# Two loading queues in the head of a two-layer GELU kernel, and three stores cut in halves

## The chip, the cores and the metric

The kernel runs on one core of one Trainium2 chip. The metric is the device time in microseconds (us). Each execution also has a span, from the first to the last instruction of the program. The device time is the span plus something outside it.

## The reference

```python
x: 16 x 512 x 768, w1: 768 x 3072, b1: 3072, w2: 3072 x 768, all float32
y = np.matmul(x, w1) + b1
y = 0.5 * y * (1.0 + erf(y / np.sqrt(2.0)))      # exact GELU
return np.matmul(y, w2).astype(np.float32)
```

## The kernel before

Both products are done with Strassen-like sums of blocks in float16. Nearly all of the run is one unbroken stream of matmuls.

The **head** loads the first four row tiles of x and the first weight tile in float32. SyncE issues them; VectorE casts them to float16. Each x tile is 128 x 768 x 4 bytes (384 KB), each half of the weight tile is as large.

```python
        for t in range(4):
            nc.sync.dma_start(out=xf[:, t, :], in_=xr[:, t, :])
        wts[0] = slots[0]
        for half in range(2):
            r = slice(half * KQ, (half + 1) * KQ)
            nc.sync.dma_start(out=wf[:, r, :], in_=w1r[:, r, 0:2 * P])
        nc.scalar.dma_start(out=bf, in_=b1.rearrange("(hc p) -> hc p", p=P))
        ...
        nc.gpsimd.tensor_copy(out=xh_of(0, 4)[:, 0:1], in_=xf[:, 0, 0:1])   # GpSimd waits for x tile 0
        load_wt(1)                       # then loads, casting on the way: the second weight tile,
        for t in range(4, 8):            # x tiles 4 to 7, and more weight tiles
            load_x(0, t)
        ...
        spin(9)                          # nine matmuls on zeros: warm-up filler for TensorE
        for t in range(4):
            xhs[t] = xh_of(0, t)
            nc.vector.tensor_copy(out=xhs[t], in_=xf[:, t, :])              # cast
            transpose_pe(0, t, copy_halves if t == 3 else nc.scalar.copy)   # 6 transposes, ScalarE copies
            if t == 0:
                nc.tensor.transpose(out=bW[:, 0:2 * NH], in_=bf, ...)       # the bias
            spin(2)
        for r, c in (...):               # three casts of the weight tile: first half in two, then the second
            nc.vector.tensor_copy(out=w1_raw(wts[0])[:, r, c], in_=wf[:, r, c])
        # ... the matmuls of the first weight tile ("plain") follow
```

The **stores** of parts of W2 (for later use) wait in a list; `drain` issues some of them at each slot of a row unit of the second product:

```python
        def raw_w2(p):
            b11, _, b21, b22 = quarters(p)
            for n, b in ((1, b11), (2, b21), (3, b22)):
                raws.append(lambda p=p, n=n, b=b: nc.sync.dma_start(out=w2s[p, n][:], in_=b))
        ...
            drain(slot, 3 if U == 0 and slot > 1 else int(U + 1 == NU))
```

The **end**: the last two pieces of output are stored by SyncE and ScalarE, one each:

```python
                (nc.sync, nc.scalar)[t].dma_start(out=orr[:, self.sb * 8 + 2 + t, N2:N2 + N4], in_=o)
```

After it, SyncE waits for every DMA semaphore that is in use. The DMAs of SyncE and ScalarE take eight semaphores in a cycle.

Of the kernel before, what the change touches and what calls it, by code (L numbers as in the profile page):

```python
# [10 lines left out]
P = 128  # L11
# [11 lines left out]
def kernel(  # L23
# [8 lines left out]
    nc = tc.nc  # L32
# [10 lines left out]
    NU = RH // P  # L43

    xr = x.rearrange("b (s p) k -> p (b s) k", p=P)
    orr = out.rearrange("b (s p) n -> p (b s) n", p=P)
    w1r = w1.rearrange("(kc p) c -> p kc c", p=P)
    w2r = w2.rearrange("(hc s p) n -> p s hc n", s=2, p=P)

    NQ = NH // 2  # L50
# [8 lines left out]
    w2s = {(p, q): dp.tile([P, NQ, N4], F16, name=f"w2s{p}{q}")  # L59
           for p in range(1, 8) for q in range(1, 8)}  # L60
# [28 lines left out]
    def cut(off, n, pattern=None, **dims):  # L89
        ap = arena[:, off:off + n]  # L90
        return ap.rearrange(pattern, **dims) if pattern else ap
# [23 lines left out]
    def wt_at(off):  # L115
        return cut(off, WT_N)
# [14 lines left out]
    slots = dict(enumerate([wt_at(o_wt + k * WT_N) for k in range(3)] + [wt_at(o) for o in o_far]))  # L131
# [73 lines left out]
    with tc.manual_schedule():  # L205
# [9 lines left out]
        def sums(ns):  # L215

            for q in (soon, queue):
                while q and ns >= q[0][0] * 0.6:
                    ns -= q[0][0]
                    q.pop(0)[1]()  # L220

        def flush(q):
            while q:
                q.pop(0)[1]()


        wts = {}
# [36 lines left out]
        puts, raws, LAG = [], [], [2]  # L264

        def quarters(p):
            w = w2v[SLOT[p]]
            return w[:, 0, 0:NQ, :], w[:, 1, 0:NQ, :], w[:, 0, NQ:NH, :], w[:, 1, NQ:NH, :]

        def split_w2(p, t, q=None, ns=(7, 5, 6, 4)):  # L270

            b11, b12, b21, b22 = quarters(p)

            def put(q, src, eng=nc.sync):
                eng.dma_start(out=w2s[p, q][:], in_=src)

            t = {n: spare[k] for n, k in zip((7, 5, 6, 4), t)}
            for n, a, b in ((7, b22, b12), (5, b12, b11), (6, b22, t[5]), (4, b21, t[6])):
                def f(n=n, a=a, b=b):
                    tt(t[n], a, b, SUB)  # L280
                    puts.append([LAG[0], lambda eng: put(n, t[n], eng)])
                if n in ns:
                    later(WB, f, slow if q is None else q)
# [5 lines left out]
        def raw_w2(p):  # L289
            b11, _, b21, b22 = quarters(p)  # L290
            for n, b in ((1, b11), (2, b21), (3, b22)):
                raws.append(lambda p=p, n=n, b=b: nc.sync.dma_start(out=w2s[p, n][:], in_=b))

        ORDER = (1, 6, 2, 7, 5, 4, 3)
        w2_order = [(ORDER[0], q) for q in (1, 2, 5, 6)]
# [53 lines left out]
        def g_sum(k, U, c0=0, c1=NH, q=None):  # L349
            G1, G2 = g_of(U // NU)  # L350
            r = slice(U % NU * P, (U % NU + 1) * P)
            g11, g21 = G1[:, c0:c1, 0, r], G1[:, c0:c1, 1, r]
            g12, g22 = G2[:, c0:c1, 0, r], G2[:, c0:c1, 1, r]
            s = [t[:, c0:c1, :] for t in GS]
            a, b, op = ((g21, g22, ADD), (s[0], g11, SUB), (g11, g21, SUB), (g12, s[1], SUB))[k]
            later((c1 - c0) * P, lambda: tt(s[k], a, b, op), q)
# [27 lines left out]
        def lev_sums(i, c0=0, c1=NQ, ks=(0, 1, 2, 3), q=None, m=None):  # L384

            A = OPERAND[ORDER[i]] if m is None else operand(*HYBRID[m])
            levs = None if m is None else hyb_lev[m]
            a11, a12 = A[:, c0:c1, 0:2 * P], A[:, NQ + c0:NQ + c1, 0:2 * P]
            a21, a22 = A[:, c0:c1, 2 * P:RH], A[:, NQ + c0:NQ + c1, 2 * P:RH]
            s = [t[:, c0:c1, :] for t in (lev_of(i) if levs is None else levs)]  # L390
            for k in ks:
                a, b, op = ((a21, a22, ADD), (s[0], a11, SUB), (a11, a21, SUB),
                            (a12, s[1], SUB))[k]
                later((c1 - c0) * 2 * P, lambda k=k, a=a, b=b, op=op: tt(s[k], a, b, op), q)
# [344 lines left out]
        xf = cut(GR, 8 * K).bitcast(FP32).rearrange("p (t k) -> p t k", t=4)  # L739
        wf = cut(GR + 8 * K, 8 * KQ * P).bitcast(FP32).rearrange("p (k c) -> p k c", c=2 * P)  # L740
        bf = cut(GR + 8 * K + 8 * KQ * P, 2 * P).bitcast(FP32)[0:2 * NH, :]
        idf = cut(GR + 8 * K + 8 * KQ * P + 2 * P, 2 * P).bitcast(FP32)
        assert 8 * K + 8 * KQ * P + 4 * P <= GR // 2
        for t in range(4):
            nc.sync.dma_start(out=xf[:, t, :], in_=xr[:, t, :])
        wts[0] = slots[0]
        for half in range(2):
            r = slice(half * KQ, (half + 1) * KQ)
            nc.sync.dma_start(out=wf[:, r, :], in_=w1r[:, r, 0:2 * P])
        nc.scalar.dma_start(out=bf, in_=b1.rearrange("(hc p) -> hc p", p=P))  # L750
        zero = XTs[1][:, 0]
        nc.vector.memset(zero[:, 0, :], 0.0)
        nc.scalar.activation(out=zero[:, 1, 0:1], in_=zero[:, 0, 0:1], func=GELU)
# [204 lines left out]
        def drain(slot, n=0, eng=nc.sync, wait=True):  # L958
            for f in puts:
                f[0] -= 1  # L960
            while puts and not (wait and puts[0][0] > 0):
                puts.pop(0)[1](eng)
            for f in raws[:n]:
                f()
            del raws[:n]

        def fill_mm2_one(sb, U, slot):
            if slot == 1:
                flush(queue)
                g_sum(2, U, q=soon)  # L970
                if U == 0:
                    g_sum(3, U, q=soon)
                flush(soon)
                if U == 0:
                    for p in (1, 2, 3, 5, 6, 7, 4):
                        raw_w2(p)
                    w4 = (6, 4, 5, 3)
                    split_w2(4, w4, ns=(5, 6, 4))
                    split_w2(1, (0, 1, 2, 6))
                    split_w2(2, (3, 0, 1, 2))  # L980
                    split_w2(4, w4, ns=(7,))
            drain(slot, 3 if U == 0 and slot > 1 else int(U + 1 == NU))
            if slot == 2:
                soon.extend(late)
                late.clear()
                if U + 1 < NU:
                    g_sum(0, U + 1, q=soon)
            if slot == 3 and U > 0:
                g_sum(3, U, q=soon)
            if slot == 4 and U + 1 < NU:  # L990
                g_sum(1, U + 1, q=soon)
            if U + 2 == NU and slot == 5:
                lev_sums(None, m=0, ks=(0, 1, 3))
            if U + 1 == NU and slot == 4:
                lev_sums(None, m=0, ks=(2,))
            if slot > 1:
                sums(1200)
            if slow and (U and slot > 1 or slot > 4):
                slow.pop(0)[1]()
                if slow and slot == 6:  # L1000
                    slow.pop(0)[1]()
            if slot == 6 and U + 1 == NU:
                flush(slow)
                flush(queue)
# [131 lines left out]
        for g, (kind, sb, k) in enumerate(units):  # L1136
            if g < 2:
                loads_a(g)
                if g:
                    transposes_a(g)  # L1140
                continue
            cur = kind(g, sb, k)
            if g < len(seq):
                period(cur, prev, lambda slot: fill_a(g, slot))
            else:
                f = {Unit1: fill_mm1, Unit2: fill_lean if sb else fill_mm2_one, UnitH: fill_hyb,
                     Unit3: fill_mm2_two}[kind]
                period(cur, prev, lambda slot: f(sb, k, slot))
            prev = cur
# [30 lines left out]
```

## Time and profile before

| what | value |
|---|---|
| time, median of the first three runs | 852.35 us (851.21 to 852.37) |
| profiled execution: time, span | 850.89, 848.7 us |
| TensorE busy | 843.3 us, 99% |
| first real matmul (line L788) | 9.39 us |
| end of TensorE to end of the span | 3.86 us |
| TensorE gaps after 9.39 us | none in busy time (the ends of matmuls are modelled; by their starts, one wait of 0.1 us at 10.8) |

To read it: a kernel whose TensorE is 99% busy can win only before its first real matmul, after its last one, or in gaps of the stream. The last two rows and the first matmul are those three places. The prediction shows the lines.

### The profile page before, as it was taken

The numbers are of one execution on the slowest core, as the hardware profiler recorded it, in microseconds if no ns is written. First come the engines' busy times: TensorE is split into PE (matmuls) and PEld (weight loads), VectorE is DVE, ScalarE is ACT, GpSimd is POOL, SyncE is SP. The second block draws the span as 40 slices with busy tenths as digits, with TensorE's granted clock in tenths as the row PEclk, the third lists the DMA queues.
The fourth block names the chain that finished last, engine by engine and source line by source line (L and its number), as shares of the span: only waits on it lengthen the run. The fifth ranks groups of instructions, "written<-read, shape, count | busy, mean of one in ns | idle before, by whom it ended". The sixth has DMA issues, their size and how long they took to land.

```text
span 848.7 us, 16767 instructions
## 1 busy us (share of the span) xinstructions
PE 843.3 (99%) x6546; PEld 577.6 (68%) x6546; DVE 673.5 (79%) x1134; ACT 426.4 (50%) x700; POOL 94.9 (11%) x151
## 2 busy tenths in 40 slices
PE   9999999999999999999999999999999999999998
PEld 5444445796544897449964499545995469964798
DVE  5766679777857997679967799668996699957997
ACT  4777763231287413773247721587116761277611
POOL 5021100042200002000020000200002100010000
PEclk9999999999999999999999999999999999999999
DMA  9998796699998699987999489994999949984397
GB/s 228 216 274 166 166 221 232 233 201 221 361 329 206 207 341 370 255 201 259 335 368 300 118 296 346 359 276 123 319 356 335 281 114 324 369 300 168 106 308 282
DMA packets 144819, 222.11 MB, mean 262 GB/s; under 512 B 61964, under 2 KB 85444, under 8 KB 144740
## 3 DMA queue, kind: packets, MB, share of 16 engines
q1 hardware_dynamic: 117392, 178.85, 66.4%
q0 software_dynamic: 27168, 42.08, 22.4%
q8 instruction: 51, 0.84, 0.4%
q14 instruction: 28, 0.23, 0.1%
q10 hardware_dynamic: 180, 0.11, 0.0%
HBM read 181.78 MB, written 49.45 MB: 272 GB/s over the span
## 4 chain that ended last, share of the span: by engine, by line
PE 99%; DMA 1%; SPq 0%; DVE 0%; ACT 0%; issue 0%
PE bY L416 22%; PE bY L520 15%; PE bX L416 14%; PE bX L520 10%; PE bZ L416 7%; PE bW L416 7%; PE bZ L520 5%; PE bW L520 5%; PE bY L459 4%; PE bZ L459 2%; PE bW L459 2%; PE bY L608 2%; PE bX L608 1%; PE bX L459 1%; DMA arena<-in_x_dram 1%; PE bZ L608 1%
## 5 line engine op out<-in xcount | busy, mean ns | idle before, releaser
L210 DVE TENSOR_TENSOR arena<-arena 128x1536 f16<-128x1536 f16 (+6 forms) x638 | 409.8, 674 | 4.8 <-DMA arena<-arena 0.7
L416 PEld LDWEIGHTS <-arena 128*128 128x128 f16 x2016 | 196.6, 98 | 220.1 <-issue 0.5
L520 PEld LDWEIGHTS <-arena 128*128 128x128 f16 x3528 | 292.1, 98 | 8.2
L416 PE MATMUL bY<-arena 128*128 128x512 f16 (+1 forms) x864 | 214.5, 375 | 0.0
L639 DVE TENSOR_TENSOR arena<-bY,arena 128x512 f32<-128x512 f32 (+1 forms) x102 | 69.4, 680 | 118.2 <-PE bY L416 88.3
L632 ACT COPY bY<-bX 128x512 f32<-128x512 f32 (+1 forms) x145 | 79.6, 549 | 118.1 <-DVE arena L569 87.8
L520 PE MATMUL bY<-arena 128*128 128x192 f16 x1500 | 138.3, 246 | 0.0
L416 PE MATMUL bX<-arena 128*128 128x512 f16 (+1 forms) x576 | 138.3, 375 | 0.0
L432 ACT ACTIVATE arena<-arena,b1t 128x1024 f16<-128x1024 f32 x94 | 108.0, 1149 | 51.6 <-DVE arena L667 51.6
L652 ACT COPY arena<-bW 128x512 f32<-128x512 f32 (+1 forms) x149 | 81.9, 550 | 93.1 <-PE bW L520 43.9
L520 PE MATMUL bX<-arena 128*128 128x192 f16 x1020 | 93.1, 246 | 0.0
L667 DVE TENSOR_TENSOR arena<-bZ,arena 128x512 f32<-128x512 f32 (+1 forms) x102 | 69.2, 679 | 22.3 <-PE bZ L416 19.1
L416 PE MATMUL bZ<-arena 128*128 128x512 f16 (+1 forms) x288 | 76.2, 375 | 0.0
L416 PE MATMUL bW<-arena 128*128 128x512 f16 (+1 forms) x288 | 76.2, 375 | 0.0
L552 POOL DMA_DIRECT2D out_dram<-arena x42 | 30.5, 728 | 403.1 <-DVE arena L663 367.5
L683 ACT COPY bZ<-bY 128x512 f32<-128x512 f32 (+1 forms) x60 | 31.8, 529 | 80.8 <-PE bY L459 30.0
L437 ACT ACTIVATE arena<-bX,b1t 128x512 f16<-128x512 f32 x94 | 64.0, 681 | 9.8 <-PE bX L416 9.7
L437 ACT ACTIVATE arena<-bY,b1t 128x512 f16<-128x512 f32 x94 | 63.3, 674 | 0.0
L459 PEld LDWEIGHTS <-arena 128*128 128x128 f16 x432 | 42.2, 98 | 28.0 <-issue 0.2
L319 POOL DMA_DIRECT2D arena<-in_x_dram x60 | 33.7, 635 | 161.7 <-DMA arena<-arena 153.4
L520 PE MATMUL bZ<-arena 128*128 128x192 f16 x504 | 48.4, 246 | 0.0
L520 PE MATMUL bW<-arena 128*128 128x192 f16 x504 | 48.4, 246 | 0.0
(63 smaller groups left out, 426.8 us busy)
## 6 DMA issues: line engine op xcount, KB each, us to landing
arena<-w2s SPq DMA_DIRECT2D x299, 288.0 KB, 4.8
arena<-w1s SPq DMA_DIRECT2D x72, 672.0 KB, 7.0
out_dram<-arena POOLq DMA_DIRECT2D x46, 384.0 KB, 7.1
w2s<-arena SPq DMA_DIRECT2D x49, 288.0 KB, 4.5
arena<-in_x_dram POOLq DMA_DIRECT2D x60, 192.0 KB, 7.6
w1s<-arena SPq DMA_DIRECT2D x12, 672.0 KB, 5.9
arena<-in_w_dram POOLq DMA_DIRECT2D x17, 384.0 KB, 8.6
out_dram<-arena SPq DMA_DIRECT2D x13, 384.0 KB, 2.5
```

What stands on the lines that cost most here:

```text
L210: nc.vector.tensor_tensor(out=o, in0=a, in1=b, op=op)
L319: nc.gpsimd.dma_start(out=xhs[t], in_=xr[:, sb * 8 + t, :])
L416: nc.tensor.matmul(out=dst[:, r:r + w], lhsT=w1_op(self.wt, slot)[:, c, :], rhs=a[:, c, r:r + w], start=first and c == 0 and r == 0, stop= ...
L432: nc.scalar.activation(out=self.G[1][:, hi, :, :], in_=self.tmp, func=GELU, bias=b1t[:, 2 * hi + 1:2 * hi + 2])
L437: nc.scalar.activation(out=self.G[0][:, hi, row, :], in_=bank[:, 0:RH], func=GELU, bias=b1t[:, 2 * hi:2 * hi + 1])
L459: nc.tensor.matmul(out=dst[:, 0:N2], lhsT=a, rhs=w[:, :, c, :], start=first and c == 0, stop=c == self.C - 1, skip_group_check=True)
L520: nc.tensor.matmul(out=dst[:, t * N4:(t + 1) * N4], lhsT=a, rhs=w[:, c, :], start=first and c == 0 and t == ts[0], stop=c == NQ - 1, skip_ ...
L608: nc.tensor.matmul(out=dst[:, t * N4:(t + 1) * N4], lhsT=a, rhs=self.w[q][:, c, :], start=first and c == 0 and t == 0, stop=c == NQ - 1, s ...
L632: nc.scalar.copy(out=bY[u.g % 2][:, 0:u.F], in_=bX[u.g % 2][:, 0:u.F])
L639: nc.vector.tensor_tensor(out=u.c22(), in0=bY[u.g % 2][:, 0:u.F], in1=w[:, 0:u.F], op=ADD)
L652: nc.scalar.copy(out=w[:, 0:u.F], in_=bW[:, 0:u.F])
L667: nc.vector.tensor_tensor(out=u.c12(), in0=bZ[:, 0:u.F], in1=w[:, 0:u.F], op=ADD)
```

## The change

The intent is a shorter head: x tiles 1 and 3 and the second half of the weight tile are issued by ScalarE while SyncE issues the others. Three of the raw W2 stores (those of product 4) go out in halves, two pieces per slot.

```diff
             for n, b in ((1, b11), (2, b21), (3, b22)):
-                raws.append(lambda p=p, n=n, b=b: nc.sync.dma_start(out=w2s[p, n][:], in_=b))
+                for c in (slice(0, NQ // 2), slice(NQ // 2, NQ)) if p == 4 else (slice(0, NQ),):
+                    raws.append(lambda p=p, n=n, b=b, c=c: nc.sync.dma_start(out=w2s[p, n][:, c, :],
+                                                                             in_=b[:, c, :]))
 ...
+        wts[0] = slots[0]
+        pair = (nc.sync, nc.scalar)
         for t in range(4):
-            nc.sync.dma_start(out=xf[:, t, :], in_=xr[:, t, :])
-        wts[0] = slots[0]
+            pair[t % 2].dma_start(out=xf[:, t, :], in_=xr[:, t, :])
+            if t == 1:
+                nc.scalar.dma_start(out=bf, in_=b1.rearrange("(hc p) -> hc p", p=P))
         for half in range(2):
             r = slice(half * KQ, (half + 1) * KQ)
-            nc.sync.dma_start(out=wf[:, r, :], in_=w1r[:, r, 0:2 * P])
-        nc.scalar.dma_start(out=bf, in_=b1.rearrange("(hc p) -> hc p", p=P))
+            pair[half].dma_start(out=wf[:, r, :], in_=w1r[:, r, 0:2 * P])
 ...
-            drain(slot, 3 if U == 0 and slot > 1 else int(U + 1 == NU))
+            drain(slot, 3 if U == 0 and slot > 1 else 2 * int(U + 1 == NU))
```

## The prediction

> **What bounds the kernel now.** I read the page first (busy time, then the chain that ended last), then that chain in order of time for the first 30 us, then the timeline of VectorE, ScalarE and the DMA issues, then the busy time by stretches.
>
> ```profile
> PE 843.3 (99%) x6546; PEld 577.6 (68%) x6546; DVE 673.5 (79%) x1134; ACT 426.4 (50%) x700; POOL 94.9 (11%) x151
> ...
> PE 99%; DMA 1%; SPq 0%; DVE 0%; ACT 0%; issue 0%
> ```
>
> TensorE is busy 843.3 us of a span of 848.7, so 5.4 us are not matmuls. In the trace's TensorE records I find 1.19 us before its first instruction, 3.86 us after its last (the final sum and stores), and three gaps of 0.17, 0.09 and 0.14 us, all before 9.39 us. From 9.39 us to 844.9 us there is no gap at all. Part of the busy time before 9.39 us is filler ("spin" matmuls on zeros), so the real margin is the head, and only the head:
>
> ```profile
> 2.14 5.54 DMA arena<-in_x_dram
> 7.68 0.02 issue
> 7.70 0.57 DVE arena L772
> 8.27 0.05 issue
> 8.32 0.52 PE bT L333 x6
> 8.84 0.02 issue
> 8.87 0.49 ACT arena L329
> 9.35 0.04 issue
> 9.39 0.81 PE bX L788 x3
> ```
>
> These are pieces of the chain: start, duration, what. The reader is to see that x row tile 3 lands at 7.68, is cast (0.57), transposed (0.52), copied by half (0.49), and the first real matmul starts at 9.39. A second path arrives at the same moment:
>
> ```profile
> 4.03 0.56 DVE L772 CAST arena<-arena 128x768 f16<-128x768 f32 x1 [2.89 <-DMA arena<-in_x_dram]
> 4.98 0.92 DVE L772 CAST arena<-arena 128x768 f16<-128x768 f32 x1 [0.39 <-DMA arena<-in_x_dram]
> 6.67 0.56 DVE L772 CAST arena<-arena 128x768 f16<-128x768 f32 x1 [0.77 <-DMA arena<-in_x_dram]
> 7.70 0.56 DVE L772 CAST arena<-arena 128x768 f16<-128x768 f32 x1 [0.47 <-DMA arena<-in_x_dram]
> 8.81 1.92 DVE L780 CAST arena<-arena 128x384 f16<-128x384 f32 x3 [0.55 <-DMA arena<-in_w_dram]
> ```
>
> From VectorE's timeline: x tiles 0 to 3 land at about 4.00, 4.96, 6.64 and 7.68 (each cast starts 0.02 to 0.03 later), the first half of W1 tile 0 at 8.79; the trace has the second half at 9.87. The first weight cast (0.43 us) ends at 9.24, so the weight path is ready some 0.1 us before the x path. Both bind. The six loads are 384 KB each (393 kB).
>
> What limits those landings is not the issue. SyncE issues the six in 0.41 to 0.49 us each, 0.74 to 3.58 us, while the first lands at 4.00. The stretches show the transfer rate:
>
> ```profile
> 2.50:4.50 2.00, 2.00 (x6) 0.70 (x5) 0.47 (x1) 0.37 (x2) 0.44 (x1) 1.00 1.08 397
> 4.50:6.50 2.00, 2.00 (x17) 1.22 (x16) 1.01 (x2) 0.82 (x2) 2.00 (x4) 1.00 0.94 300
> 6.50:8.50 2.00, 1.74 (x18) 0.75 (x16) 1.12 (x2) 1.53 (x3) 2.00 (x4) 1.00 1.05 369
> ```
>
> Last two columns: DMA share and GB/s. The engines are full from 2.5 us (share 0.94 or more). One 3072-byte packet takes 121 ns in the packet records, so 16 engines give 16 x 3072 / 121 = 406 GB/s: the 397 seen is the limit. Between 4.5 and 6.5 us some packets take 300 to 1100 ns and the rate falls to 300, a loss of (397 - 300) x 2 us = 194 kB or 0.5 us.
>
> **What the Trainium skill says.** (1) "DMA: Bandwidth & Descriptors", section "Issuing engines are not separate DMA queues": initiating DMAs on several engines only saves the sequencer's time to initiate them. The trace agrees in that 6 issues of 0.45 us are 2.7 us in all and end well before the data. (2) Same page, "Queues, rings and completion order": each DMA engine takes the queue rows it has work for in turn, a packet at a time. The trace of before can't show it for SyncE against ScalarE (ScalarE's only early load is 12 KB of bias). For SyncE against GpSimd it does not agree: GpSimd's first load, issued at 4.57, has its first packet at 8.60, when SyncE's are running out. (3) "ScalarE: Activation LUTs", "What ACT_TABLE_LOAD costs": about 1283 ns; the trace has 1.28 us. (4) "TensorE: Matmul & The Clock Gate", "Part 1": after an idle window of about 3.4 us the clock halves. Before, no idle comes near that.
>
> **The change, part by part.**
>
> *Head, issue.* ScalarE now issues x1, the bias, x3 and the second weight half: 3 x 0.45 + 0.62 us, with 0.05 between, from 0.73 to about 2.8 us. Its table load then moves from 1.39 to about 2.8 and ends near 4.1, with the tiny GELU 4.3; ScalarE's first copy is at 5.68 before. This costs nothing. SyncE's last head issue ends at about 2.1 instead of 3.58; nothing waited for it. Saving on the path: at most the start-up. Before 2.5 us only 94 GB/s x 0.5 us flow; [...]an estimated 0 to 0.15 us.
>
> *Head, order.* The bytes stay 6 x 393 kB, the engines stay full, so the last of the six still lands near 9.87. But two queues served in turn carry two tiles side by side: x0 and x1 both arrive near 4.9 (instead of 4.00 and 4.96), x2 and x3 both near 7.6 (instead of 6.64 and 7.68), and both weight halves near 9.7 to 9.85 (instead of 8.79 and 9.87). The half needed first loses what the other does not gain: it is about 0.9 us later. Then:
> weights: 9.7 + 0.02 + cast 0.43 + 0.05 to TensorE = 10.2.
> x: x2 cast from 7.6, x3 cast 8.15 to 8.7, transposes to 9.2, ScalarE's copies of tile 2 (0.80, from 8.65) and the half of tile 3 (0.49) to 9.95.
> The first real matmul starts at about 10.2 instead of 9.39: +0.8. Given back: before, the second weight half's cast ended at 10.73 and the matmul that needs it began at 10.79 to 10.85 instead of 10.69, so about 0.1 of waiting vanishes (after, the casts end at 11.2 and the second half is needed at 10.2 + 1.3 = 11.5). With the start-up gain of 0.05: net about +0.65 us. If the slow stretch of 4.5 to 6.5 us goes, 0.5 of it comes back: +0.15.
>
> *Behind the head.* GpSimd waits for x0 before it issues W1 tile 1 and x4 to x7; with x0 0.9 later its issues move from 4.57 to about 5.4. Their data start only as the six loads end, so they land as before: 11.65, 12.60, 13.57, 14.53, 15.46 in the trace. TensorE used them at 12.10, 12.71, 13.62, 14.57 and 16.24. So a head that is later has no new wait there; a head that is earlier has 0.05 to 0.4 us of room, unless these loads move too.
>
> *The three raw W2 stores in halves.* SyncE issues nine instead of six pieces in the last of the four row units of the second matmul, two per slot instead of one:
>
> ```profile
> 149.58 2.56 SPq L292 DMA_DIRECT2D w2s<-arena  x3
> ...
> 156.12 0.43 SPq L292 DMA_DIRECT2D w2s<-arena  x1
> ...
> 158.33 0.97 SPq L292 DMA_DIRECT2D w2s<-arena  x2
> ```
>
> Three more issues of about 0.45 us, where the queue idles 3.5 us at a time (its longest wait for an output), and where TensorE runs without a gap: 0 us. I take the purpose to be the count: three loads left SyncE's queue and three stores join it, so all later DMAs on SyncE use the semaphores that they used before (the trace shows them reused in a cycle of eight). Between the head and this place the cycle is shifted by three; the waits for reuse recorded there had all been met early.
>
> Sum: +0.65 to +0.15 us, no other part. 0.65 of 852 is 0.08%.
>
> **Rivals.** (a) *Real gain*: two queues keep each engine supplied across the stalls, or the slow stretch is the single queue's. Then all six land by about 2.3 + 2359 / 406 = 8.1 us at best, the first weights near 8.2, x3 near 6.3, and the head is up to 0.7 us shorter; GpSimd's loads, which follow, would move with it. For it: the loss of 194 kB sits at the border of the second and third load. Against: single packets are slow there, which another queue on the same engine doesn't cure. It would give about 851.5. (b) *One queue goes first*, as GpSimd's did not get its turn: then x0, x2 and the first weights land by about 6.9, but x3 only at about 8.8, and 1.7 us of cast, transpose and copy follow: first matmul at 10.5, +1.0: 853. (c) *Clock*: TensorE idles more between 5 and 10 us, and the clock could fall to half, which would cost up to an estimated 1.7 us (half of 3.4): 854. Against: the spins remain and idle stretches stay near 1 us. (d) *Hidden anyway*: 0, since the rest is gapless but the head's waits cancel.
>
> **Range and chances.** The three times of before scatter by 1.2 us (851.21 to 852.37), more than the effect, and the profiled run took 850.89; the mean of the four is 851.7. Adding 0.65, less a share for rival (a), gives 852.2; the median quoted for before is 852.35, which would give 852.8. I say 852.4. Mechanism (-0.7 to +1.0) and scatter (about 0.6 either way) give 851.0 to 853.7. Two per cent is 17 us: no path here moves that, for the whole head is 9.4 us.
>
> **What would show it.** Right: x0's cast near 4.9 with x1's directly behind, x2 and x3 together near 7.6, the first weight cast at 9.6 or later and the matmuls of L788 starting at about 10.2; no TensorE gap after them; nothing changed around 145 to 165 us except nine short stores. Wrong: a first weight half that lands at 8.8 or earlier (then the sharing step failed), a rate over 390 GB/s from 4.5 to 6.5 us (rival a), x3 after 8.5 (rival b), warm-up matmuls of 0.42 us spacing after 9 us (rival c), or new gaps at the transposes of x4 to x6.

## The result, and the profile after

| | before | after |
|---|---|---|
| median of six runs of each | 852.05 us | 850.57 us |
| lowest to highest | 850.84 to 852.55 | 850.20 to 850.88 |
| ratio of the mean of fast runs | | 0.9985, interval 0.9972 to 0.9998 |
| profiled span | 848.7 | 848.6 |

Ratios here are the mean time of one kernel's fast runs over that of the other's in the same rounds, so they are not quite the ratio of the medians quoted. The change gained about 1.3 us, a small but real gain; the prediction had 852.4 in a range of 851.0 to 853.7, and its sum was a loss of 0.15 to 0.65 us. It was wrong.

The profile of the changed kernel, in the same views. First, the page's busy line and its line of ScalarE's DMA queue:

```profile
PE 842.7 (99%) x6546; PEld 577.6 (68%) x6546; DVE 673.3 (79%) x1134; ACT 426.4 (50%) x700; POOL 95.0 (11%) x151
...
q10 hardware_dynamic: 868, 1.29, 0.4%
```

ScalarE's queue moved 1.29 MB (before 0.11), as intended. Then the chain in order of time (start, duration, what):

```profile
1.83 6.01 DMA arena<-in_x_dram
...
7.87 0.73 DVE arena L776
...
8.64 0.52 PE bT L335 x6
...
9.19 0.49 ACT arena L331
...
9.72 0.81 PE bX L792 x3
```

The reader is to see that the chain is still the one of x tile 3, now issued by ScalarE at 1.83, and that in this execution the first real matmul is at 9.72, 0.33 us *later* than in the profiled execution of before. Yet the span is 0.1 shorter. VectorE's timeline has the casts:

```profile
5.04 1.88 DVE L776 CAST arena<-arena 128x768 f16<-128x768 f32 x3 [3.91 <-DMA arena<-in_x_dram]
7.87 0.72 DVE L776 CAST arena<-arena 128x768 f16<-128x768 f32 x1 [0.95 <-DMA arena<-in_x_dram]
8.85 1.42 DVE L784 CAST arena<-arena 128x384 f16<-128x384 f32 x3 [0.26 <-DMA arena<-in_w_dram]
```

x0 and x1 land together (5.01 and 4.80 in the trace), x2 follows at once (5.92), x3 lands at 7.84, the weight halves at 8.82 and 9.39. And the transfer rate, by the same stretches as before (last column, GB/s):

```profile
2.50:4.50 2.00, 2.00 (x6) 0.71 (x5) 0.00 (x0) 1.49 (x2) 0.00 (x0) 1.00 0.96 362
4.50:6.50 2.00, 1.27 (x11) 0.59 (x10) 1.46 (x3) 0.30 (x1) 1.43 (x2) 1.00 1.01 378
6.50:8.50 2.00, 1.90 (x18) 1.05 (x16) 1.05 (x2) 1.84 (x4) 2.00 (x5) 1.00 1.08 366
```

The slow stretch of before (300 GB/s from 4.5 to 6.5 us) is nearly gone. Around the stores, the DMA issues of SyncE:

```profile
149.68 4.78 SPq L293 DMA_DIRECT2D w2s<-arena  x6
...
156.22 0.95 SPq L293 DMA_DIRECT2D w2s<-arena  x2
...
158.43 0.43 SPq L293 DMA_DIRECT2D w2s<-arena  x1
```

Nine pieces instead of six, and TensorE has no gap there, nor anywhere behind 9.72 us.

### The profile page after: what moved, and what is told of

It is laid out like the page before. It is cut to its first block, busy times and chain, and to the rows that moved or that the text cites. A ratio compares the mean times of both kernels' runs of the same rounds, so it can differ in the third digit from the quotient of the medians.

```text
span 848.6 us, 16771 instructions
## 1 busy us (share of the span) xinstructions
PE 842.7 (99%) x6546; PEld 577.6 (68%) x6546; DVE 673.3 (79%) x1134; ACT 426.4 (50%) x700; POOL 95.0 (11%) x151
## 3 DMA queue, kind: packets, MB, share of 16 engines
q10 hardware_dynamic: 868, 1.29, 0.4%
## 4 chain that ended last, share of the span: by engine, by line
PE 98%; DMA 1%; DVE 0%; ACTq 0%; ACT 0%; issue 0%
PE bY L418 22%; PE bY L522 15%; PE bX L418 14%; PE bX L522 10%; PE bZ L418 7%; PE bW L418 7%; PE bZ L522 5%; PE bW L522 5%; PE bY L461 4%; PE bZ L461 2%; PE bW L461 2%; PE bY L610 2%; PE bX L610 1%; PE bX L461 1%; DMA arena<-in_x_dram 1%; PE bZ L610 1%
```

## The experiments

The two traces do not explain 1.3 us: their spans differ by 0.1. Theories at the start: **A**, the head is what gains, through arrival times that differ from execution to execution; **B**, the gain lies in the stores, in the end, or outside the span. Fifteen kernels ran, in four groups; those of one group ran on one chip beside runs of the kernel before.

### 1. The kernel before again, each half of the change alone, and a narrower head

`b_again` is the kernel before with a comment added.

> The kernel before once more, unchanged but for a comment, for the spread of its spans and a second trace. Theory A (the head's arrival times vary from execution to execution under one queue): spans spread over about 1.5 us, and in the new trace the first real matmul differs from 9.39 us by as much as the span differs from 848.7. Theory B (the time lies outside the span, or later in the stream): spans within 0.3 us of each other, or the first real matmul at 9.4 us with a longer span. The median should be 851.5 to 852.5 either way.

`head_only` is the changed kernel with `if p == 0` in place of `if p == 4` (no store is cut) and one store per slot.

> The head of the change, the W2 stores whole and one per slot as before. Theory A (all of the gain is the head's): 850.6 us, ratio 0.9985, spread under 1 us. Theory B (the stores, or the place of later loads in the cycle of semaphores, give it): 851.5 to 852.4, ratio 0.999 to 1.001.

`stores_only` is the kernel before with the two hunks of the stores.

> The three stores in halves, the head as before. Theory A: as before, ratio 1.000 within 0.001, with the spread of before. Theory B: ratio 0.9985, about 850.6 us.

`x_split_only` is the changed kernel with both weight halves on SyncE:

```diff
-            pair[half].dma_start(out=wf[:, r, :], in_=w1r[:, r, 0:2 * P])
+            nc.sync.dma_start(out=wf[:, r, :], in_=w1r[:, r, 0:2 * P])
```

> The change without the second weight half on ScalarE's queue: both halves follow each other on SyncE's behind x0 and x2. By the sharing step the first half then lands ahead of the second, about 8.3 us, and the x path alone (x3 at 7.8) sets the first matmul: near 9.7 us as in the changed kernel, where the weights came 0.4 us before the x path. Theory A: equal to the changed kernel within 0.3 us, 850.6. If the placing of the weight half matters: 851.5 or more.

Measured, five runs each and nine of before (median 851.43, mean 851.51):

| kernel | median us | mean us | spans | time outside the span, mean |
|---|---|---|---|---|
| b_again | 851.55 | 851.62 | 849.1 to 850.0 | 2.14 |
| head_only | 850.98 | 851.17 | 848.7 to 849.8 | 2.15 |
| stores_only | 850.99 | 851.05 | 849.0 to 849.6 | 1.79 |
| x_split_only | 852.13 | 851.57 | 848.6, 848.9, and 850.4 to 850.5 three times | 1.81 |

The intervals of the ratios all hold 1.0 (head_only 0.9996, 0.9983 to 1.0008; stores_only 0.9995, 0.9982 to 1.0009), so times alone settle nothing. The last column does: every execution of the kernels without cut stores has 2.08 to 2.20 us outside its span, every one with them 1.72 to 1.84. So theory B has a part that doesn't depend on the head: **0.35 us outside the span**.

b_again's trace fits neither theory as written: its span is 1.0 us longer than the first trace's, its first real matmul (9.68) only 0.28 later. By the starts of the matmuls, most of the rest is in two waits behind the head: 0.38 us at 13.4, and 0.40 at 481.6, where a load lands late (chain in order of time):

```profile
473.49 8.06 DMA arena<-w1s
...
481.60 0.82 PE bX L417 x3
```

The traces show a second part of theory B, at the end of the span. SyncE's waits after 844 us (total us, times, longest), kernel before, then stores_only:

```profile
SPq L1175 <- DMA out_dram<-arena: 1.9, 3, 1.1
```

```profile
SPq L1177 <- DMA out_dram<-arena: 1.6, 2, 1.1
```

These are the waits for the DMA semaphores at the end. In the trace's records SyncE goes through them in a fixed order, some 0.06 us each when there is nothing to wait for. The last store to land is ScalarE's, 2.71 and 2.70 us after TensorE's last matmul. Before, its semaphore is the fourth of the eight, and four more waits of 0.06 follow it; with three more DMAs issued in between, it is the seventh, and one follows. TensorE's end to the end of the span: 3.86 us before, 3.85 in b_again and head_only, 3.68 in stores_only, 3.67 in the changed kernel. That is **0.18 us**.

x_split_only has two kinds of execution. The trace is of a long one; its chain in order of time:

```profile
5.79 0.82 PE bT L335 x6
...
7.80 0.64 PE bT L335 x6
...
9.29 0.64 PE bT L335 x6
...
10.55 0.35 PE bT L335 x6
...
11.45 0.81 PE bX L792 x3
```

Six transposes take 0.64 us and, after 10.2 us, 0.35: the granted clock is half up to 10.18 us. Then the head is bound by TensorE's own transposes and filler, and the first real matmul is 1.7 us later than in the changed kernel. The prediction's rival (c) is real, though not in the changed kernel's own trace (its clock rises at 4.50).

### 2. The place in the cycle, GpSimd's start, the bias, more filler

`stores_plus8` cuts more stores of the kernel before (product 4 in thirds, two of product 7 in halves, three pieces per slot), eight more DMAs in all.

```diff
+                k = 3 if p == 4 else 2 if p == 7 and n < 3 else 1
+                for c in [slice(i * NQ // k, (i + 1) * NQ // k) for i in range(k)]:
```

> The kernel before with eight more pieces of raw W2 stores (the three of the fourth product in thirds, two of the seventh in halves) instead of three more. The cycle of DMA semaphores has eight places, so eight more leave the last DMA at the place it had before. Theory P (the place in the cycle sets the tail): as before, 3.86 us from TensorE's last instruction to the end of the span, the last load's wait followed by four more waits, and 2.15 us of the time outside the span. Theory C (finer or earlier stores, or the count): 3.67 us and 1.80 us as with three more.

Measured: median 851.15, ratio 0.9997 (0.9985 to 1.001); 2.11 to 2.15 us outside the span; end of TensorE to end of the span 3.85 us; SyncE's waits after 844 us:

```profile
SPq L1178 <- DMA out_dram<-arena: 1.9, 3, 1.1
```

All three are back at the values of before. Finer, earlier and more numerous stores gain nothing by themselves; what fits is their number modulo eight (0, 3 and 8 more were tried). Theory P holds, for the tail in the span and for the 0.35 us outside it, whose mechanism no trace shows.

`pool_wait_x1` lets GpSimd start later in the kernel before:

```diff
-        nc.gpsimd.tensor_copy(out=xh_of(0, 4)[:, 0:1], in_=xf[:, 0, 0:1])
+        nc.gpsimd.tensor_copy(out=xh_of(0, 4)[:, 0:1], in_=xf[:, 1, 0:1])
```

> The kernel before, but GpSimd waits for x tile 1 instead of x tile 0 before it issues its loads, so it issues at about 5.5 us as in the changed kernel, with all six loads still on one queue. Theory G (the slow stretch of the six loads, 79 to 104 kB in the half microsecond from 5.5, comes of GpSimd's issuing): the stretch moves about 1 us later or shrinks, and the mean span falls by 0.2 to 0.4 us. Theory Q (it is the single queue's): the stretch stays at 5.0 to 6.3 us and the mean span stays 849.4 within 0.2.

Measured: 851.36, ratio 0.9998 (0.9985 to 1.001), spans 848.9 to 849.4, mean 849.14 beside 849.29. The stretch from 5.5 to 6.5 us is no longer slow (178 and 197 kB per half microsecond in the packet records), but 4.0 to 5.5 is (162, 153, 159). So a slow stretch remains, earlier rather than later: neither theory as written. What the six loads had moved by 6.5 us was 1473 kB, in the middle of the other traces with one queue and under all those with two. Delaying GpSimd does not give what two queues give.

`bias_later` puts the bias behind x3 on ScalarE's queue:

```diff
-            if t == 1:
+            if t == 3:
                 nc.scalar.dma_start(out=bf, in_=b1.rearrange("(hc p) -> hc p", p=P))
```

> The changed kernel with the bias load behind x3 on ScalarE's queue, so that x3 is issued at about 1.15 us instead of 1.83, before the first weight half on SyncE's queue (1.68). If loads of both queues are served in the order of their issue (in the changed kernel's trace they are), x3 lands near 6.8 us instead of 7.84, the x path is then bound by the chain of ScalarE's copies from x0, first matmul near 9.35 us instead of 9.72, and the span is 0.2 to 0.4 us shorter. If the queues are served in turn whatever the issue time, x3 lands at 7.6 or later and nothing changes.

Measured: 853.33, ratio 1.0023 (1.001 to 1.0037): slower. x3 did land at 6.93 instead of 7.84, and x2 at 7.29. So an earlier issue did bring x3 in earlier. The order of issue is not the whole rule, though: in the changed kernel the first weight half, issued at 1.68 us, lands at 8.82, behind x3, issued at 1.83 and landed at 7.84 (the part on the prediction says why). And I had overlooked that TensorE transposes the bias after the first x tile, and the bias now came later. TensorE's timeline:

```profile
5.93 0.82 PE L335 MATMUL bT<-ident,arena 128*128 128x128 f16 x6 [0.72 <-POOL arena L760]
7.66 0.27 PE L779 MATMUL bW<-arena 24*128 24x24 f32 x1 [0.91 <-DMA arena<-in_b_dram]
```

With 0.7 and 0.9 us of idling the clock stayed at half until 13.67 us, and the first real matmul came at 13.17.

`spin12` is the changed kernel with `spin(12)` for `spin(9)`.

> The changed kernel with twelve warm-up matmuls instead of nine, so that TensorE is busy up to about 5.4 us and the gap before the first transposes shrinks from 0.73 to under 0.3 us. Theory K (executions in which the clock turns to full only at 10 us, as in the trace of the x-only split, are those whose activity window held this gap): no span over 849.8 in five rounds. If the gap is not the cause: slow ones of about 850.4 still occur. The fast ones stay at 848.4 to 849.1.

Measured: 850.62, ratio 0.9991 (0.9978 to 1.0003), spans 848.8 to 849.1, no long one. In its trace the clock rose early (3.85 us), x0 landed late (5.44), and the gap was still 0.84 us; so it did not test what it was made for, beyond showing that a gap after the rise does no harm.

### 3. The old order on two queues, the changed kernel again, and the gap once more

`order_kept` issues bias, x2 and the first weight half on ScalarE, the others on SyncE.

```diff
+        nc.scalar.dma_start(out=bf, in_=b1.rearrange("(hc p) -> hc p", p=P))
+        for t, eng in enumerate((nc.sync, nc.sync, nc.scalar, nc.sync)):
+            eng.dma_start(out=xf[:, t, :], in_=xr[:, t, :])
+        for half, eng in enumerate((nc.scalar, nc.sync)):
```

> The changed kernel with its three stores in halves, but the head's loads placed so that the order of issue stays as before: bias, x2 and the first weight half on ScalarE's queue, x0, x1, x3 and the second weight half on SyncE's. Served in the order of issue, x0 lands alone near 4.0 us again, x1 near 5.0, x2 near 6.0, x3 near 7.2, the first weights near 8.2; first matmul near 8.9 us, span 848.2, time 850.0, and no gap of TensorE near 5 us, so no execution with a late clock. If two queues are served in turn, x3 and the first weights land near 7.8 and 8.9 as in the changed kernel and the span is 848.8.

> The changed kernel once more. From its parts measured apart (head 0.35 us, stores 0.46 us of the mean time) it should be about 0.8 us under the kernel before, 850.5 to 850.8, with spans of 848.5 to 849.1 and 1.8 us outside them; more (1.3 us as in the first comparison) if the two parts help each other. Some execution may have the late clock (span near 850.4).

`x_split_spin12` is x_split_only with `spin(12)`.

> The x-only split with twelve warm-up matmuls instead of nine. With nine, three of five executions had a span of 850.4 to 850.5 and two 848.6 to 848.9, and the trace of a long one has TensorE at half clock up to 10.18 us, after a gap of 0.58 us in its filler at 5.2. Twelve at half clock last to about 6.3 us and close that gap. Theory K (an activity window that holds the gap doesn't release the clock): no span over 849.8 in five, all of 848.6 to 849.4. If the gap isn't the cause: long ones of 850.4 remain.

Measured, five runs each (six of x_split_spin12), beside eleven of before (median 851.65, mean 851.79, spans 848.8 to 851.1):

| kernel | median us | ratio (interval) | spans |
|---|---|---|---|
| order_kept | 850.79 | 0.9990 (0.9978 to 1.0002) | 848.8 to 849.4 |
| after_again | 850.52 | 0.9986 (0.9973 to 0.9999) | 848.5 to 849.4 |
| x_split_spin12 | 850.77 | 0.9994 (0.9983 to 1.0006) | 848.7 to 849.3, and one of 851.6 |

after_again confirms the first comparison: 1.2 us less in the mean, again more than the 0.8 that I had added up from the parts. order_kept brought x0 at 4.09 and x3 at 7.36, but the first weights, which now shared the engines with the second half, at 9.01 (halves 0.25 us apart); first real matmul 9.52. It does not beat the changed kernel, and I found no version that does. x_split_spin12 had one long execution in six where x_split_only had three in five; its trace, with no gap near 5 us, has the clock rise at 4.79. That fits theory K as far as it goes, but the one of 851.6 was forbidden by it, and no trace of that one exists. The clock records of all 17 traces add a hint: the stretch at full clock lasts 839.68, 843.09 or 846.50 us and nothing else, so its two ends lie on steps of 3.41 us. A rise that is missed would come a whole step later, which fits theory K, but the records don't show what decides it. Theory K is not settled.

The trace of after_again (span 849.4, the longest of its five) shows a bound behind the first matmul, in TensorE's timeline:

```profile
13.66 0.49 PE L336 MATMUL bT<-ident,arena 128*128 128x128 f16 x6 [0.26 <-DMA arena<-in_x_dram]
```

That is x tile 4, loaded by GpSimd, landing at 13.53 instead of 12.55. order_kept (0.23 us) and x_split_spin12 (0.22) wait at the same place.

### 4. Looking for a long execution of before

> The kernel before, one look for a trace. Spans of before were 848.8 to 849.7 in most executions and 849.9 to 851.1 in about one of five. Theory K: if this one is long, its clock turns to full later than 5.3 us and its first real matmul is later than 10 us. Theory L: if it is long, its loads landed late (x3 after 8.3 or GpSimd's first load after 12.6) under a clock that turned by 5.3.

> As the first look: span 848.8 to 849.7, or long with a late clock (theory K) or late landings (theory L).

> As the first look: span 848.8 to 849.7, or long with a late clock (theory K) or late landings (theory L).

`b_spin4` is the kernel before with `spin(4)`.

> The kernel before with four warm-up matmuls instead of nine, so that TensorE is idle from about 2.9 to 4.6 us. Theory K: the clock turns to full only near 7 to 10 us; six transposes and two fillers per x tile take 1.5 us instead of 0.76, the first real matmul comes 1 to 2 us later, and spans are 850.5 to 851.1, like the long executions of before. If the clock matters little: spans of 849 to 849.7.

Measured: the three looks had spans of 849.1, 849.4 and 849.2, none of them long, so they could not tell K from L. b_spin4 (three rounds): median 851.69, ratio 1.0002 (0.9986 to 1.0019), spans 849.3 to 850.1. In its trace (850.1) the clock rose at 8.56 us, the first real matmul came at 10.18, 0.1 to 0.8 us later than in the five traces of before. So a late clock costs less in the head of before than in the head with two queues: x3 lands at 8.15 there anyway. That expectation was too high.

The looks were useful for something else: five traces of the kernel before instead of one. b_look2's chain in order of time shows a gap that the first trace did not have (start, duration, what):

```profile
36.88 5.09 DMA arena<-arena
...
43.32 0.71 DVE bZ L686
...
44.08 0.81 PE bY L417 x3
```

The last transposing DMA of a group lands at 41.97; VectorE's work behind it lets TensorE go on only at 44.08. By the starts of the matmuls all three looks lose 0.22 to 0.24 us there. The first trace and b_again do not; nor do those of after, after_again and head_only. But spin12, which has the changed head and three more filler matmuls, loses 0.30 us at the same place:

```profile
43.13 0.71 DVE bZ L687
...
43.89 0.81 PE bY L418 x3
```

So do b_spin4, pool_wait_x1 and stores_plus8 with the old head (0.31 to 0.38), but not stores_only. In all, six of nine traces with one queue have this wait, and one of eight with two: the changed head makes it rarer at most, it does not remove it.

## Why the prediction was wrong

**The baseline.** It took the head of one trace as the head of the kernel. The 44 executions of before whose spans are known beside the profiled one (on four chips) have a mean span of 849.42 and a median of 849.3 us; the profiled one had 848.7. First real matmul in five traces of before: 9.39, 9.68, 9.69, 10.06, 9.34. The landings of the weights that the sum starts from (8.79 and 9.87) are the earliest of the five, one tied.

**"Head, order", the step that gave +0.8, failed.** It had the two queues deliver side by side all the way, equal bytes to each, with the same end as before. x0 and x1 did come together (5.01 and 4.80; I said 4.9). But x2 came at 5.92, not 7.6, and the first weights at 8.82, not 9.7. x3 came at 7.84, near the 7.6 of the text; the second weights at 9.39, not 9.85. In x_split_only, head_only and after_again the first weights land at 8.94, 8.73 and 9.07: always before the step's 9.7. ScalarE's queue had nothing in the engines from about 4.6 to 5.4 us, although x3 was issued by 2.19; so SyncE's queue had them to itself. bias_later shows that the bias's place between x1 and x3 has to do with it. Why the wait was so long stays open.

What the step said of turns was right, but they are turns of packets. Where both queues have work, the packet records show about as many packets of each: 29 and 28 from 3.0 to 3.5 us in bias_later (x tiles on both queues, 3072 bytes each), 95 and 95 from 7.0 to 7.5 (weights on both, 1024 bytes each). In the changed kernel x3 meets the first weight half: 52 packets of 1024 bytes on SyncE's queue from 6.5 to 7.0 us, 53 on ScalarE's, 40 of them of 3072. So x3 took most of the bytes and landed first, though issued later. The first weight half still came 0.9 us earlier than the step had it, since x2 had gone ahead alone.

The signs that the prediction set for its being wrong were narrowly missed: 8.82 where it said "at 8.8 or earlier", and 378 GB/s from 4.5 to 6.5 us where it said over 390.

**"The engines stay full, so the last still lands near 9.87" failed too.** This is rival (a), to which I gave a small share. The busy share misled: it was 0.94 at 300 GB/s, as a packet that takes 300 to 1100 ns counts as busy for all of it. The packet records of the nine traces with one queue have 1352 to 1544 kB moved by 6.5 us (mean 1452), those of the eight with two 1542 to 1665 (mean 1614). In five traces of before the last packet of the six loads starts at 9.45 to 9.72 us, in after, after_again and head_only at 8.67 to 9.09. GpSimd's first packet, which still comes only as they run out, starts at 8.42 to 8.73 against 8.09 to 8.26. So two queues feed the engines better: some 160 kB (bias counted), or an estimated 0.4 us at 400 GB/s. By 2.5 us the means are 126 kB and 95, so most of it is the slow stretch. order_kept, where GpSimd issues at 4.66 us as before, has the most of all (1665 kB), so GpSimd's later start is not what did it.

**Yet the first matmul gained nothing.** The three traces with the changed head have it at 9.72, 9.96 and 9.35, mean 9.68; the five of before have a mean of 9.63. x3 lands at 7.62 to 8.11 in the one and 7.62 to 8.09 in the other. So the right size of this step is about 0, not +0.65: as I read it, the better feed is spent on x0 arriving 1 us later and on x3 waiting behind the bias (order_kept, free of both, was bound by the first weights instead: 9.52).

**"Behind the head, as before": half right.** GpSimd's issues moved by 1 us without harm, as said. What I missed is that its loads come earlier as a series: the last weight load of the series, issued at 24 us, lands at 35.61 to 36.19 against 35.95 to 36.62, 0.3 us earlier in the mean, with overlap. The five traces of before show waits at 10.8 to 11.1 (about 0.1 us, three of them), near 13 (0.31 and 0.38), near 44 (0.22 to 0.24, three) and at 481.6 us (0.40, b_again); the three of the changed head only near 13 (0.25 and 0.44), but spin12 has the one near 44. From the first real matmul to the last, the mean is 835.51 us in five traces of before, 835.29 in three of the changed head. That is 0.2 us in a few traces, of which b_again's late load alone makes 0.08: an indication rather than a proof.

**"The three raw W2 stores in halves: 0 us" failed.** This is the largest part that is certain. I took the purpose to be that SyncE's count of DMAs stays the same. But SyncE and ScalarE take their semaphores from one cycle: both heads issue seven DMAs from it, and SyncE's next has the same place in both. So the head shifts nothing (head_only: 3.85 us and 2.15), and the three new stores shift everything behind them by three. What that buys is at the end: 0.18 us in the span, 0.35 us outside, 0.53 us together. stores_plus8 shows it: eight more pieces take both away again.

**The sum as measured.** Mean span of before 849.42; of after and after_again, eleven executions, 848.80: a difference of 0.62, of which 0.18 is the tail. So the head is worth an estimated 0.44 in the mean span (0.3 if medians are compared; 0.35 for head_only beside its own rounds, whose interval holds no change). The traces place some 0.2 of that behind the first matmul and nothing before it; the rest is not located. And 0.44 + 0.18 + 0.35 = 0.97 us, where the two direct comparisons gave 1.3 and 1.2, in rounds where the kernel before had more long executions. Five of its 44 spans are 850.0 to 851.1; none of the eleven is over 849.4. What makes those long ones, and whether the change prevents them or was lucky, stays open: no trace caught one.

**What held.** Nothing changed in the stream around 145 to 165 us. ScalarE's table load moved to 2.70 us at no cost. GpSimd's later start was harmless. No run came near a change of 2%. The rival of the clock was named, with 1.7 us as an estimate: x_split_only has just that between its two kinds of execution, and bias_later more.

## What to carry to other kernels

When the end of a program waits for its DMA semaphores in a fixed order, the place of the last store in their cycle is worth looking at: a few more or fewer DMAs anywhere before it can move it. Before a change of a microsecond is judged, take several traces of the kernel before: here the first showed a head that three of five traces did not have. And two queues can fill the DMA engines better while the tile that is needed first arrives later, so look at each landing, not at the sum.

## What the Trainium skill lacked or had wrong

- "DMA: Bandwidth & Descriptors", "Issuing engines are not separate DMA queues": it says that issuing from several engines only saves the sequencer's time. In this head two queues had moved 1614 kB by 6.5 us in the mean of eight traces, one queue 1452 in the mean of nine, though every issue was done by 3.7 us in all of them.
- The same page, "Queues, rings and completion order": it has each engine take its queues in turn, packet by packet. Between SyncE's and ScalarE's queues the packet records agree while both have work (29 and 28 packets, 95 and 95). GpSimd's queue got no such turn: its first packet came at 8.60 us after an issue at 4.57, as SyncE's loads ran out (8.09 after 5.58 with two queues). What held ScalarE's x3, issued by 2.19 us, until 5.45, with the bias before it on the queue, the page does not tell.
- "TensorE: Matmul & The Clock Gate", "Part 1": it has a busy window of about 3.4 us raise the clock, and does not say how short a gap spoils one. Here a gap of 0.41 us before the rise (after_again) went with a rise at 6.30 us, and gaps of 0.58 us (x_split_only), 1.75 (b_spin4), and 0.72 and 0.91 (bias_later) with one at 10.18, 8.56 and 13.67; the 13 traces without such a gap have 3.85 to 6.02. A gap of 0.84 us after the rise (spin12) did no harm.
- None of the pages used here has the order of the waits at the end of a program: some 0.06 us for each semaphore behind that of the last store, and 0.35 us outside the span that went with it (2.08 to 2.20 us against 1.72 to 1.84).
